# Splitting a 128-place expert's second-stage weights while the 64-place expert behind it runs its first stage

## The chip, the cores and the metric

The kernel runs on one core of a Trainium2 chip. The metric is the device time in microseconds (us) from launch to end, as a median of several runs. An execution under the profiler gives a trace; its span runs from the first to the last instruction. The tensor engine (PE) multiplies, the scalar engine (ACT) and the vector engine (DVE) work on tiles, POOL gathers and scatters rows, and SP issues the weight loads.

## The reference

A two-layer backbone over 256 latent and 256 context tokens: a mixer (convolutions in layer 0, latent attention in layer 1), then a mixture of 16 experts, of which each token takes two.

```
def hier_moe(h, wg, bg, we, be, w1, w3, w2):
    ...
    for e in range(N_EXPERTS):
        hid = jax.nn.silu(t @ w1[e]) * (t @ w3[e])
        out = out + gates[:, e:e + 1] * (hid @ w2[e])
```

D_MODEL is 1024 and D_EXPERT 512, so an expert has 6 MB of weights: w1 and w3 for the first stage, w2 for the second. All is float32.

## The kernel before, in words

The experts of a layer are ranked by the tokens they got and run one after the other. The order of ranks is SEQ; below, a number such as 7 or 8 is the place i in SEQ. The first ranks ("128-place", called B) take up to 128 tokens, the later ones ("64-place", called s) up to 64. In layer 0, places 1 to 10 alternate B, s; then 11 and 12 are B, 13 s, 14 B, 15 s. In layer 1, places 1 to 8 alternate B, s and 9 to 15 are all s. A pair is a B and the s behind it: (1,2), (3,4), (5,6), (7,8), (9,10), (12,13), (14,15) in layer 0 and (1,2), (3,4), (5,6), (7,8) in layer 1.

A B expert multiplies with three products of float32r halves: each weight tile of 1 MB is *split* (L80 to L102) into two column halves, and for each half ACT casts a rounded copy (`wh`, L93) and DVE subtracts it from the source (`wl`, L94). PE then runs `wh` by the high part (L105), `wh` by the low part of the other operand (L106 in the order of the rows) and `wl` by the high part (L107). The split buffers are rings of four `wh` and four `wl` halves, that is of two weight tiles. An s expert multiplies its weights as they are, in float32: L800 in the first stage, L826 in the second.

Each expert has six loads, issued by SP in the order in which the code asks for them: four of the first stage (w1 and w3, two halves of the contraction each) and two of the second (w2). They go into 11 slots of 1 MB, used in turn (`wr` 7 of them, `wx` 4), so that a load waits until the slot's last user, a split or the last L800 or L826 of a tile, is done.

The loop over i (L987 and on) is staggered: it runs the first stage of expert i (`ffn_in` or `ffn_in_half`), and only then the second stage of i-1 (`out_e(i - 1)`, which calls `down` or `down_half`). In between the four weight tiles of the first stage, a list of steps `between` is run, one behind each tile: first `hid`, the transposed hidden row of i-1 (L773 with ACT's L775 and DVE's L776, or L813 with L815), then the transposes of the tokens of i+1 (L699 with L700, or twice L709 with L711 and L712). The second stage's result is weighted by the gate on ACT in layer 0 (`y`, L933), on DVE in layer 1 (L931), and scattered by POOL. L806 and L807 form the hidden row of an s expert from both banks of its first stage.

What order the instructions of an engine have in the program is decided by a scheduler that goes by the code's order and its own estimate of when things are ready. On the chip each engine keeps that order.

Of the kernel before, what the change touches and what calls it, by code (L numbers as in the profile page):

```python
# [44 lines left out]
def backbone(ctx: ExitStack, tc: tile.TileContext, I, out):  # L45
# [13 lines left out]
    def pt(shape=(128, 512)):  # L59
        return pp.tile(list(shape), F32, name="pt", tag="pt", bufs=2)  # L60

    def py(shape=(128, 512)):
        return pp.tile(list(shape), F32, name="py", tag="py", bufs=2)
# [10 lines left out]
    def scratch(t=None):  # L74

        if t is None:
            t = "wh" if scr_n[0] % 2 == 0 else "wl"
            scr_n[0] += 1
        return ring.tile([128, 1024], F32, name="scr", tag=t, bufs=NSPL)
# [5 lines left out]
    def split(src, n=2048):  # L85

        m = n // 2
        hl = []
        for i in range(2):
            hi = ring.tile([128, 1024], F32R, name="wh", tag="wh", bufs=NSPL)  # L90
            lo = ring.tile([128, 1024], F32R, name="wl", tag="wl", bufs=NSPL)
            x = src[i] if isinstance(src, list) else src[:, i * m:(i + 1) * m]
            S.copy(hi[:, :m], x)  # L93
            V.tensor_tensor(lo[:, :m], x, hi[:, :m].bitcast(F32), op=ALU.subtract)  # L94
            hl.append((hi, lo))

        def at(o, width):
            i, o = divmod(o, m)
            return [t[:, o:o + width] for t in hl[i]]

        return at

    def mm3(ps, a, b, start, stop):

        T.matmul(ps, a[0], b[0], start=start, stop=False)  # L105
        T.matmul(ps, a[1], b[0], start=False, stop=False)  # L106
        return T.matmul(ps, a[0], b[1], start=False, stop=stop)  # L107
# [671 lines left out]
    def down(hT, loads):  # L779

        hh, hl = hT
        po = [py(), py()]
        for kh in range(2):
            cur = split(loads.pop(0)())
            for k in range(2):
                kk = kh * 2 + k
                for h in range(2):
                    o = k * 1024 + h * 512
                    mm3(po[h], (hh[:, kk, :], hl[:, kk, :]), cur(o, 512), kk == 0, kk == 3)
        return po  # L790
# [78 lines left out]
    def overflow(l, R, xg, mp):  # L869

        v = nc.values_load(R.mx[0:1, 0:1], min_val=0, max_val=R.nch * 128)
        with tc.If(v > 128, preferred_fallthrough_block=False):

            R.fill()
            posb = sp.tile([128, 2, R.nch], F32, name="posb", tag="posb")
            idc = mp.tile([128, 2, 1], I32, name="idc")
            gtc = mp.tile([128, 1], F32, name="gtc")
            V.tensor_tensor(posb, R.posk, R.cap, op=ALU.add)
            with tc.For_i(0, R.nch, 1):
                V.tensor_scalar(posb, posb, -128.0, None, op0=ALU.add)  # L880
                t = slots(R, posb, "1")
                with tc.For_i(0, NE, 1) as e:
                    V.tensor_copy(idc[:, 0, :], t.idg[:, bass.ds(e, 1)])
                    V.tensor_copy(idc[:, 1, :], t.ids[:, bass.ds(e, 1)])
                    V.tensor_copy(gtc, t.gate[:, bass.ds(e, 1)])
                    win, wout = weights(l, e, lambda: mp.tile([128, 1024], F32, name="wo", tag="ya", bufs=2), True)
                    gather(R, xg, idc[:, 0, :])
                    xb = list(gather_T(xg, mp))[1]
                    hb = ffn_in(xb, win, lambda: scratch()[:, :FE])
                    scatter(R, weigh(R, down(hidden_T(hb, mp), wout), gtc, scratch()), idc[:, 1, :])  # L890

    def new_hs(mp, l):
        return lambda: mp.tile([128, FE], F32, name="hs", tag="hs", bufs=2 - l)

    def experts(l, R, after, mid=None):
# [3 lines left out]
        with tc.tile_pool(name=f"mp{l}", bufs=1, reuse_waits="tile") as mp:  # L899
# [5 lines left out]
            small = [r >= NBIG[l] for r in seq]  # L905
            gate = lambda i: R.t0.gate[:, seq[i]:seq[i] + 1]

            def gat(i):
                idx = R.t0.idg[:, seq[i]:seq[i] + 1]
                if small[i]:  # L910
                    gather_half(R, XG[i % 2][:, :512], idx)
                else:
                    gather(R, XG[i % 2], idx)

            def tokens_T(i):
                return gather_half_T(R, XG[i % 2][:, :512], mp) if small[i] else gather_T(XG[i % 2], mp)
# [22 lines left out]
            def out_e(i):  # L939
                rows_out(i, (down_half if small[i] else down)(hT.pop(i), wout[i]))  # L940

            win, wout, hs, hT = {}, {}, {}, {}
# [45 lines left out]
            for i in range(1, NE):  # L988
                if i < NE - 1:
                    gat(i + 1)  # L990

                def hid():
                    hT[i - 1] = (hidden_half_T if small[i - 1] else hidden_T)(hs.pop(i - 1), mp)

                between = [hid]
                xs = []
                if i < NE - 1:
                    g = tokens_T(i + 1)
                    step = lambda: xs.append(next(g))
                    between += [step] if small[i + 1] else [step, step]  # L1000
                hs[i] = (ffn_in_half if small[i] else ffn_in)(x, win[i], new_hs(mp, l), between)
                x = xs[-1] if xs else None
                out_e(i - 1)
                if i == 2:

                    for j in range(NLAST):
                        sl = scratch()
                        ps = pt((128, nch, 128))
                        r = seq[NE - NLAST + j]
                        for c in range(nch):  # L1010
                            o = sl[:, c * 128:(c + 1) * 128]
                            if r < NBIG[l]:
                                V.tensor_scalar(o, iot1, R.pe[:, c, r:r + 1], None, op0=ALU.is_equal)
                            else:
                                V.tensor_scalar(o.rearrange("p (h n) -> p h n", h=2), iot64, R.pe[:, c, r:r + 1], None, op0=ALU.is_equal)
                            T.transpose(ps[:, c, :], o, ident)
                        S.copy(selT[:, j, :], ps.rearrange("p c n -> p (c n)"))
# [333 lines left out]
    with tc.tile_pool(name="lp", bufs=1, reuse_waits="tile") as lp:  # L1351
        odd.qc = lp.tile([128, 2, 384], F32, name="qc")
        experts(0, R0, after0, odd_q)
        for g in (1, 2):
            shuffle(1, g)
        R1 = odd_layer(A1, B1)
    experts(1, R1, finish)


# [71 lines left out]
```

## Time and profile before

| what | value |
|---|---|
| time, median of 3 runs | 1008.94 us (1007.98 to 1009.62) |
| the profiled execution's own time | 1010.3 us |
| its span | 1008.5 us |
| PE busy (matmuls) | 911.0 us, 90% |
| DVE busy | 595.8 us, 59% |
| ACT busy | 392.3 us, 39% |
| granted PE clock, mean | 0.959 |
| HBM traffic | 320 GB/s over the span |

The experts of layer 0 lie from about 290 to 570 us of the span and those of layer 1 from about 750 us to the end. A row of the timeline gives the start, the length, the engine, the line and what was done; in brackets, how long the engine had been idle and what ended that. Rows of several instructions (x48) are merged.

### The profile page before, as it was taken

The numbers are of one execution on the slowest core, as the hardware profiler recorded it, in microseconds if no ns is written. First come the engines' busy times: TensorE is split into PE (matmuls) and PEld (weight loads), VectorE is DVE, ScalarE is ACT, GpSimd is POOL, SyncE is SP. The second block draws the span as 40 slices with busy tenths as digits, with TensorE's granted clock in tenths as the row PEclk, the third lists the DMA queues.
The fourth block names the chain that finished last, engine by engine and source line by source line (L and its number), as shares of the span: only waits on it lengthen the run. The fifth ranks groups of instructions, "written<-read, shape, count | busy, mean of one in ns | idle before, by whom it ended". The sixth has DMA issues, their size and how long they took to land. (4 is left out here: it accounts for less than half of the span.)

```text
span 1008.5 us, 13283 instructions
## 1 busy us (share of the span) xinstructions
PE 911.0 (90%) x4885; PEld 615.9 (61%) x4885; DVE 595.8 (59%) x944; ACT 392.3 (39%) x571; POOL 119.2 (12%) x127
## 2 busy tenths in 40 slices
PE   2799999999699999999999989999879999999973
PEld 0466676557587775666665468655667776655530
DVE  2789999345777564455643677675589573530005
ACT  2432211321357564355543257343257453221102
POOL 3000000040112111111001011010121111111000
PEclk9899999989899999999999889999979999999997
DMA  9998897984549999999995674262449999999993
GB/s 363 338 340 304 304 328 312 363 327 169 212 162 419 419 420 418 406 396 405 381 359 202 221 235 137 83 227 87 148 164 405 407 386 417 377 401 418 419 420 142
DMA packets 80681, 313.66 MB, mean 311 GB/s; under 512 B 8603, under 2 KB 32155, under 8 KB 50017
## 3 DMA queue, kind: packets, MB, share of 16 engines
q1 hardware_dynamic: 70032, 290.34, 74.4%
q0 software_dynamic: 6368, 11.78, 3.1%
q10 hardware_dynamic: 4208, 10.61, 2.7%
q8 instruction: 40, 0.66, 0.3%
q14 instruction: 33, 0.26, 0.1%
HBM read 301.56 MB, written 21.23 MB: 320 GB/s over the span
## 5 line engine op out<-in xcount | busy, mean ns | idle before, releaser
L94 DVE TENSOR_TENSOR wl<-wr,wh 128x1024 fp32r<-128x1024 f32 (+2 forms) x172 | 201.1, 1204 | 48.4 <-ACT wh L93 47.0
L93 ACT CAST wh<-wr 128x1024 fp32r<-128x1024 f32 (+2 forms) x172 | 172.7, 1037 | 135.1 <-PE pa L107 51.0
L105 PE MATMUL pa<-wh,xh 128*128 128x512 f32 x224 | 92.8, 414 | 5.6 <-ACT wh L93 5.2
L107 PE MATMUL pa<-wl,xh 128*128 128x512 f32 x224 | 91.2, 408 | 2.6 <-DVE wl L94 2.5
L106 PE MATMUL pa<-wh,xl 128*128 128x512 f32 x224 | 90.4, 404 | 1.2 <-DVE xl L712 1.2
L800 PE MATMUL pa<-wr,xs 128*64 128x256 f32 x720 | 84.0, 382 | 3.8 <-DMA wr<-in_moe_w 3.8
L334 DVE SCALAR_TENSOR_TENSOR ca<-apad,cols,ca 128x512 f32<-128x512 f32 x120 | 84.0, 746 | 0.8
L800 PEld LDWEIGHTS pa<-wr,xs 128*64 128x64 f32 x720 | 49.6, 137 | 32.5 <-DMA wr<-in_moe_w 6.8
L105 PE MATMUL pa<-wx,wh 128*128 128x512 f32 x160 | 63.6, 402 | 3.9 <-ACT wx L234 3.9
L183 PE MATMUL py<-wr,csil 128*32 128x512 f32 x384 | 53.2, 659 | 11.1 <-ACT csil L154 11.1
L106 PE MATMUL pa<-wx,wl 128*128 128x512 f32 x160 | 62.6, 393 | 0.0
L107 PE MATMUL pa<-wx,wh 128*128 128x512 f32 x160 | 62.6, 393 | 0.0
L94 DVE TENSOR_TENSOR wl<-wx,wh 128x1024 fp32r<-128x1024 f32 x44 | 52.1, 1220 | 5.2 <-ACT wh L93 4.5
L105 PEld LDWEIGHTS pa<-wh,xh 128*128 128x128 f32 x224 | 43.3, 193 | 18.0 <-ACT wh L93 8.9
L105 PE MATMUL py<-wh,hTh 128*128 128x512 f32 x112 | 47.1, 420 | 6.3 <-ACT wh L93 6.3
L807 DVE TENSOR_TENSOR hs<-hs,pa 128x256 f32<-128x256 f32 x18 | 7.6, 421 | 76.5 <-PE pa L800 76.5
L93 ACT CAST wh<-wx 128x1024 fp32r<-128x1024 f32 x44 | 44.7, 1051 | 19.8 <-PE pa L106 7.3
L107 PEld LDWEIGHTS pa<-wl,xh 128*128 128x128 f32 x224 | 43.2, 193 | 14.9 <-DVE wl L94 4.2
L800 PE MATMUL pa<-wx,xs 128*64 128x256 f32 x432 | 50.5, 382 | 1.1 <-DMA wx<-in_moe_w 1.1
L106 PEld LDWEIGHTS pa<-wh,xl 128*128 128x128 f32 x224 | 43.3, 193 | 11.2 <-DVE xl L712 1.8
L106 PE MATMUL py<-wh,hTl 128*128 128x512 f32 x112 | 46.0, 411 | 0.0
L105 PE MATMUL pa<-wh,wx 128*128 128x512 f32 (+1 forms) x112 | 42.6, 382 | 0.5 <-ACT wh L93 0.5
(358 smaller groups left out, 1514.2 us busy)
## 6 DMA issues: line engine op xcount, KB each, us to landing
wr<-in_moe_w SPq DMA_DIRECT2D x124, 1024.0 KB, 11.5
wx<-in_moe_w SPq DMA_DIRECT2D x68, 1024.0 KB, 11.9
wr<-in_w_mod SPq DMA_DIRECT2D x48, 1024.0 KB, 9.5
wr<-in_ev_w_in SPq DMA_DIRECT2D x20, 512.0 KB, 5.7
wr<-Y SPq DMA_DIRECT2D x6, 1024.0 KB
wr<-in_ev_w_out SPq DMA_DIRECT2D x4, 1024.0 KB
Y<-xg SPq DMA_DIRECT2D x1, 4096.0 KB
wr<-in_od_w_out SPq DMA_DIRECT2D x4, 1024.0 KB
```

Of the source, the lines that this page charges most:

```text
L93: S.copy(hi[:, :m], x)
L94: V.tensor_tensor(lo[:, :m], x, hi[:, :m].bitcast(F32), op=ALU.subtract)
L105: T.matmul(ps, a[0], b[0], start=start, stop=False)
L106: T.matmul(ps, a[1], b[0], start=False, stop=False)
L107: return T.matmul(ps, a[0], b[1], start=False, stop=stop)
L183: T.matmul(ps[32 * j:32 * j + 32, :], csil[:, l, k, :], w[:, j * 512:(j + 1) * 512], start=k == 0, stop=k == 7)
L334: V.scalar_tensor_tensor(acc, apad[:, bi, :, t:t + 256], col("caw", t * 4 + bi), acc, op0=ALU.mult, op1=ALU.add)
L800: T.matmul(ps[m][64 * h:64 * h + 64, :], x[:, k, kh * 64:kh * 64 + 64], w[:, k * 512 + h * 256:k * 512 + h * 256 + 256], start=kh == 0 and ...
L807: V.tensor_tensor(hs, hs, ps[1], op=ALU.mult)
```

## The change

Where expert i is a 64-place one and expert i-1 a 128-place one, the loop puts two steps into `between`: behind the second weight tile of i's first stage the first w2 tile of i-1 is taken and split, and behind the third tile the second. `down` then finds the finished split in place of the weights. The loads are asked for in that order too: of i the first two tiles, w2's first of i-1, i's third, w2's second, i's fourth; before it was i's four and then the two of w2.

```diff
--- before.py
+++ after.py
@@ -781,7 +781,9 @@
         hh, hl = hT
         po = [py(), py()]
         for kh in range(2):
-            cur = split(loads.pop(0)())
+            cur = loads.pop(0)()
+            if not callable(cur):
+                cur = split(cur)
             for k in range(2):
                 kk = kh * 2 + k
                 for h in range(2):
@@ -998,6 +1000,15 @@
                     g = tokens_T(i + 1)
                     step = lambda: xs.append(next(g))
                     between += [step] if small[i + 1] else [step, step]
+                if small[i] and not small[i - 1]:
+
+                    def early(kh):
+                        at = split(wout[i - 1][kh]())
+                        wout[i - 1][kh] = lambda: at
+
+                    between += [lambda: None] * (3 - len(between))
+                    b1, b2 = between[1:3]
+                    between[1:3] = [lambda: (b1(), early(0)), lambda: (b2(), early(1))]
                 hs[i] = (ffn_in_half if small[i] else ffn_in)(x, win[i], new_hs(mp, l), between)
                 x = xs[-1] if xs else None
                 out_e(i - 1)
```

No instruction is added or left out; the scheduler gives some of them other places. In the changed file the lines behind L784 stand two lines lower (L800 is L802, L806 is L808, L813 is L815, L815 is L817, L933 is L935) and those behind L1000 eleven.

On PE, pair (7,8) of layer 0 before: 8 rows from the transposes of place 9's tokens on. `py` is the second stage of 7, `pa` under L800 the first stage of 8; x8 is one weight tile.

```order
L709 MATMUL pt<-ident,xg_1962 128x128 x4
L800 MATMUL pa<-wr,xs 64x256 x8
L709 MATMUL pt<-ident,xg_1962 128x128 x4
L800 MATMUL pa<-wr,xs 64x256 x24
L813 MATMUL pt<-ident,hs 128x128 x2
L699 MATMUL pt<-ident,xg_1961 128x128 x4
L105 MATMUL py<-wh,hTh 128x512
L106 MATMUL py<-wh,hTl 128x512
```

The same place in the changed kernel:

```order
L709 MATMUL pt<-ident,xg_1962 128x128 x4
L802 MATMUL pa<-wr,xs 64x256 x8
L105 MATMUL py<-wh,hTh 128x512
L106 MATMUL py<-wh,hTl 128x512
L105 MATMUL py<-wh,hTh 128x512
L106 MATMUL py<-wh,hTl 128x512
L107 MATMUL py<-wl,hTh 128x512 x2
L105 MATMUL py<-wh,hTh 128x512
L106 MATMUL py<-wh,hTl 128x512
L802 MATMUL pa<-wr,xs 64x256 x8
L107 MATMUL py<-wl,hTh 128x512
```

Eight of the 24 second-stage matmuls of 7 now stand ahead of the third tile of 8, twelve ahead of the fourth, and four behind it; L813 (now L815) and L699 follow those.

On ACT, the same pair before, from the hidden row of 7 (L775) to the casts of place 9 (`wx`, and the last `wr` ahead of them):

```order
L775 CAST hTh<-pt 128x512
L711 CAST xh<-pt 128x512 x2
L806 ACTIVATE hs<-pa 128x256
L815 COPY hTs<-pt 128x256
L93 CAST wh<-wr 128x1024 x2
L700 COPY xs<-pt 128x512
L93 CAST wh<-wr 128x1024 x3
L933 ACTIVATE y<-py,gate_2095 128x512 x2
L93 CAST wh<-wr 128x1024
L93 CAST wh<-wx 128x1024 x6
```

In the changed kernel:

```order
L775 CAST hTh<-pt 128x512
L711 CAST xh<-pt 128x512 x2
L93 CAST wh<-wr 128x1024 x2
L808 ACTIVATE hs<-pa 128x256
L93 CAST wh<-wr 128x1024 x2
L935 ACTIVATE y<-py,gate_2095 128x512 x2
L93 CAST wh<-wr 128x1024 x2
L817 COPY hTs<-pt 128x256
L700 COPY xs<-pt 128x512
L93 CAST wh<-wx 128x1024 x6
```

The four casts of w2 moved up, two of them ahead of the activation of 8's hidden row and two behind it. The first cast of place 9, which was ahead of the two weightings of 7 (the third of the x3), is now behind them.

On DVE, the last pair of layer 0, (14,15), before; L174 shuffles modulation rows for layer 1 and has nothing to do with the experts:

```order
L776 TENSOR_TENSOR hTl<-pt,hTh 128x512
L807 TENSOR_TENSOR hs<-hs,pa 128x256
L174 STREAM_SHUFFLE modc<-modr 128x512
L94 TENSOR_TENSOR wl<-wr,wh 128x1024 x4
L866 SCALAR_TENSOR_TENSOR xl<-py,gate_2095,xh 128x512 x2
```

In the changed kernel:

```order
L776 TENSOR_TENSOR hTl<-pt,hTh 128x512
L94 TENSOR_TENSOR wl<-wr,wh 128x1024 x2
L174 STREAM_SHUFFLE modc<-modr 128x512
L94 TENSOR_TENSOR wl<-wr,wh 128x1024 x2
L809 TENSOR_TENSOR hs<-hs,pa 128x256
```

Two of the four subtractions of 14's w2 moved ahead of the shuffle, and L807 (now L809) moved behind it and behind the other two.

## Rows read from the trace of the kernel before

**Rows 1.** Windows: stretch, busy us of each engine, granted clock, DMA share, GB/s.

```profile
core 0: us, PE busy (x) PEld busy (x) DVE busy (x) ACT busy (x) POOL busy (x), PEclk, DMA share, GB/s
390.00:545.00 155.00, 143.79 (x716) 97.03 (x714) 83.74 (x83) 81.05 (x103) 16.50 (x16) 0.98 0.96 375
...
880.00:985.00 105.00, 93.57 (x670) 51.59 (x668) 14.76 (x21) 13.26 (x26) 11.21 (x12) 1.00 1.01 413
```

**Rows 2.** PE's waits from 378 to 570 us: total, times, longest.

```profile
PE pa L105 <- ACT wh L93: 5.2, 9, 1.7
PE py L105 <- ACT wh L93: 4.4, 5, 1.4
```

**Rows 3.** Timeline of PE, pair (7,8) of layer 0.

```profile
419.97 5.40 PE L800 MATMUL pa<-wr,xs 128*64 128x256 f32 x48
425.97 0.50 PE L813 MATMUL pt<-ident,hs 128*128 128x128 f32 x2 [0.59 <-DVE hs L807]
426.31 0.65 PE L699 MATMUL pt<-ident,xg 128*128 128x128 f32 x4
427.88 0.50 PE L105 MATMUL py<-wh,hTh 128*128 128x512 f32 x1 [0.92 <-ACT wh L93]
428.21 0.40 PE L106 MATMUL py<-wh,hTl 128*128 128x512 f32 x1
...
436.13 0.50 PE L105 MATMUL pa<-wh,xh 128*128 128x512 f32 x1 [0.67 <-ACT wh L93]
...
446.13 0.40 PE L106 MATMUL pa<-wh,xl 128*128 128x512 f32 x1
446.37 0.40 PE L107 MATMUL pa<-wl,xh 128*128 128x512 f32 x1
```

**Rows 4.** Timeline of ACT, the same pair.

```profile
420.08 0.59 ACT L711 CAST xh<-pt 128x512 fp32r<-128x512 f32 x1 [1.93 <-PE pt L709]
423.69 0.38 ACT L806 ACTIVATE hs<-pa 128x256 f32<-128x256 f32 x1 [3.03 <-PE pa L800]
426.51 0.37 ACT L815 COPY hTs<-pt 128x256 f32<-128x256 f32 x1 [2.43 <-PE pt L813]
426.78 2.00 ACT L93 CAST wh<-wr 128x1024 fp32r<-128x1024 f32 x2
433.88 1.27 ACT L933 ACTIVATE y<-py,gate 128x512 f32<-128x512 f32 x2 [1.78 <-PE py L107]
```

**Rows 5.** Timeline of DVE, the same pair.

```profile
427.86 5.88 DVE L94 TENSOR_TENSOR wl<-wr,wh 128x1024 fp32r<-128x1024 f32 x5 [1.94 <-ACT wh L93]
```

**Rows 6.** Loads and gathers: issues, KB each, median us from issue to landing.

```profile
wr<-in_moe_w SPq DMA_DIRECT2D x124, 1024.0 KB, 11.5
xg<-hmD,idx POOLq DMA_INDIRECT x30, 7.7
```

**Rows 7.** Timelines of PE and ACT, pair (12,13) of layer 0.

```profile
512.70 1.95 PE L800 MATMUL pa<-wx,xs 128*64 128x256 f32 x16
...
512.81 0.59 ACT L711 CAST xh<-pt 128x512 fp32r<-128x512 f32 x1 [1.97 <-PE pt L709]
```

**Rows 8.** Timelines of PE, DVE and POOL, pair (14,15), the end of layer 0's experts.

```profile
543.62 3.67 PE L800 MATMUL pa<-wx,xs 128*64 128x256 f32 x32
...
551.34 0.51 PE L813 MATMUL pt<-ident,hs 128*128 128x128 f32 x2 [0.59 <-DVE hs L807]
553.25 0.50 PE L105 MATMUL py<-wh,hTh 128*128 128x512 f32 x1 [1.41 <-ACT wh L93]
...
564.72 3.65 PE L826 MATMUL py<-wr,hTs 128*64 128x512 f32 x16
...
553.94 0.73 DVE L174 STREAM_SHUFFLE modc<-modr 128x512 f32<-128x512 f32 x1
...
551.10 1.48 POOL L214 PARTITION_BROADCAST wr<-modr  x2 [5.96 <-issue]
```

**Rows 9.** Windows at three places where the granted clock changed.

```profile
516.00:519.60 3.60, 2.08 (x13) 1.43 (x10) 1.16 (x2) 2.09 (x3) 0.00 (x0) 1.00 1.00 362
519.60:523.00 3.40, 3.40 (x10) 2.33 (x9) 3.38 (x4) 3.40 (x5) 0.00 (x0) 0.51 1.03 412
...
553.80:560.60 6.80, 5.85 (x14) 4.13 (x13) 5.24 (x6) 2.24 (x3) 0.10 (x1) 0.50 0.69 263
```

**Rows 10.** The chain that ended last, near the end: start, us, what.

```profile
964.59 20.09 DMA wr<-in_moe_w
984.68 0.14 issue
984.81 1.94 PE py L826 x8
```

## The prediction, made before the changed kernel ran

> **What bounds the kernel now.** I read first which resource is full in the two stretches that the change touches. At the end of layer 1 the transfers are: the DMA share is 1.01 and 413 GB/s move, while PE is busy 93.57 of 105 us [rows 1]; the chain that ended last runs there through a wait of 20.09 us for a weight load, and the last eight matmuls of L826 start when it has landed [rows 10]. In layer 0, from 390 to 545 us, PE is busy 143.79 of 155 us, with the DMA share at 0.96 and 375 GB/s: both are near their limit, and 11.2 us of PE are idle [rows 1]. What PE waits for there is not a load: the largest items are `pa` and `py` matmuls that wait for a cast of ACT, 5.2 us in 9 waits and 4.4 us in 5 [rows 2]. So layer 0 goes by the chain PE, ACT, DVE, PE, and layer 1's end goes by bytes.
>
> The pair (7,8) shows where these waits lie. PE does three tiles of L800 without a pause, then waits 0.59 for `hs`, transposes (L813, L699), waits 0.92 for the first split half of w2, and 0.67 for the first tile of place 9 [rows 3]. ACT explains the 0.92: between the activation of `hs` at 423.69 and the copy at 426.51 it waits 2.43 us for L813, and the two casts stand behind that copy [rows 4]. They could have run much earlier; this idle stretch of ACT is what the change fills. A cast takes 1.00 us (2.00 for two), a subtraction 1.18 (5.88 for five) [rows 4, 5].
>
> **The change, part by part.** Work is only moved. PE's second-stage rows of a pair (24 `py` matmuls) now stand 8 ahead of the third tile, 12 ahead of the fourth, 4 behind it. In layer 0 this happens in the pairs (5,6), (7,8), (9,10), (12,13) and (14,15); in (1,2) and (3,4) the scheduler had the casts and matmuls inside the first stage already, and PE's order stays. Of layer 1's pairs only (5,6) and (7,8) change, long before the loads of the end, which arrive at the pace of the DMA either way: I put them at 0, with half a us either way if the first-stage loads of their s experts, now asked for behind w2, come late.
>
> I walk pair (7,8) on durations from [rows 3 to 5]. The second tile of 8 ends at 421.77 (419.97 plus 16 of the 48 matmuls in 5.40). The casts of w2 stand behind the second copy L711 (it follows the one at 420.08 and ends at 420.67), so the halves are cast at 421.7 and 422.6, and their differences done at 422.9 and 424.1. A 512-wide matmul in a run takes 0.235 (446.13 to 446.37). PE: four to 422.7, 0.2 wait, four to 423.9, third tile 1.8 to 425.7, four more to 426.6. The activation of `hs` (0.38) can begin only at 425.8, and the third cast stands behind it: done at 427.25, so PE waits 0.6. Four to 428.2, wait 0.3 for the difference, four to 429.45, fourth tile to 431.25, last four to 432.2, L813 and L699 (0.34 and 0.65) to 433.15. ACT now has both weightings of L933 (1.27 the pair) ahead of the first cast of place 9; the second weighting needs the last `py` of 432.2 and ends at 433.0, so the cast ends at 434.0 and its difference at 435.3. PE waits 0.9, does two matmuls, waits 0.8, and the other 46 of place 9 end at 446.05. Before it was 446.6 (446.37 and one matmul): 0.55 gained.
>
> Against that stands a cost at each restart: the first wide matmul after a change takes 0.33 (427.88 to 428.21) instead of 0.235 [rows 3]. Four more changes at 0.1 are 0.4 lost; nothing is the bound on the other side. So **+0.15 a pair**, between -0.3 and +0.55. The old waits (0.59, 0.92, 0.67) go, and nearly the same amount comes back (0.2, 0.6, 0.3, 0.9, 0.8). I take this for three pairs: **+0.45**, although (5,6) may give 0.
>
> ACT keeps its order in this: the casts at 426.78 start right behind the copy at 426.51, and the next cast of place 9 could not pass L933 [rows 4]. The Trainium skill says so as a rule ("TensorE: Matmul & The Clock Gate", section "Architectural detail: the array is 16× 32×32, not 1× 128×128"): the queues of ScalarE and VectorE are strictly first in, first out. The trace agrees. Could a ready cast overtake, by estimate 2.3 us of the waits in my walk (0.6, 0.9, 0.8) would go; by the rule, they stay.
>
> Pair (12,13) has a worse start: PE is free at 512.7, when L800's sixteen begin, but w2's casts stand behind two L711 of 0.59 from 512.81 on, so that the first half is there at 514.4: 1.7 us of waiting [rows 7]. What comes behind is as in the walk. About the same stall existed there before, later on, so I put it at **-0.3**, restarts included.
>
> Pair (14,15) ends layer 0 and has no next expert, hence no L933 of a successor to suffer from. Its two middle tiles of 32 matmuls run from 543.62 for 3.67 us [rows 8], to 547.2 with what is due then. Now: eight wide matmuls to 549.1, third tile to 550.9, four to 551.8, activation to 551.3, third cast to 552.3, which is 0.5 of waiting, four to 553.25. Then the difference: on DVE it stands behind the shuffle L174, which before started at 553.94, after POOL's L214, and took 0.73 [rows 8]. So it ends at 554.7 plus 1.18, at 555.8: **2.55 us of waiting that the change brings in**. After that four to 556.8, fourth tile to 558.6, four to 559.5, and with the transposition and copy L826 starts at 561.4, if the clock stays up. Before it was 564.72, after waits of 0.59 and 1.41 and with the clock at 0.50 from 553.8 to 560.6 [rows 8, 9]. If 2.55 us of waiting bring a fall too, the start is at 563.1. The gain is 3.3 or 1.6; less 0.4 of restarts, and nearer the lower end, **+1.8**.
>
> What has cover: the s experts' third and fourth loads, one or two places later in SP's order, land 11.5 us after issue and are used a long way behind that; the token gather of 7.7 us stands behind a scatter that is now later by a few us, and its rows are wanted a pair later [rows 6]. If that cover went, each would cost up to its few us once per pair; PE's waits of before show none of that kind, so 0.
>
> **The clock.** Behind waits of 0.59 and 0.92 near 516 to 519.6 (PE busy 2.08 of 3.6), the granted clock is 0.51 for 3.4 us, that is at the lower of the two levels, 1.2 GHz [rows 9]. A fall so costs half of 3.4: 1.7 us. Yet the same two waits in pair (7,8) brought none [rows 3], and the mean clock from 390 to 545 is 0.98 [rows 1]. The skill has a matching sentence ("TensorE: Matmul & The Clock Gate", section "A second HAM failure mode: psum-queue depth-cycling"): short idles of PE between groups of matmuls can make the clock go back and forth, and each fall is paid again. The rows at 519.6 agree, those of pair (7,8) do not. The waits of the walk are as long and come closer together, so I take one fall more than before: **-1.7**; none and three are the bounds.
>
> **Sum.** 0.45 - 0.3 + 1.8 - 1.7 + 0 = 0.25 us less. On the profiled execution's own 1010.3 us (span 1008.5) that is 1010.05; it lies 1.36 above the median of 1008.94, so the median is forecast at **1008.7**.
>
> **The rivals.**
> A, faster: no added fall, and restarts that cost nothing more than the waits themselves. Then 3 x 0.55 + 0.1 + 2.2 = 3.95: **1005.0**. For it: most pairs of before run at full clock through such waits [rows 1]. Against it: the 0.33 in [rows 3].
>
> B, slower: the clock falls once more in each of the pairs (5,6), (7,8) and (9,10). It happens where the wait behind L933 (0.9 and 0.8 within some 2.5 us) comes a little longer. Three falls cost 5.1, less the 1.95 of the other terms: 3.15 slower, **1012.1**. It decides from three falls on; with two the loss is 1.45 and not measurable. For it: [rows 9]; against: the 0.59 and 0.92 without a fall.
>
> C, the change does nothing: DMA paces layer 0 too. For it the share of 0.96; against, 375 GB/s beside 413 where the DMA does bind [rows 1], and waits that name ACT [rows 2]. **1008.9**.
>
> **How the numbers follow.** 0.2%, or 2.0 us, is about what a measurement of this kernel can tell from no change. The forecast (the walks about right, and no more than two added falls) has 0.38, A 0.26, B 0.28, C 0.08. Forecast and C lie within 0.2%: faster 0.26, same 0.46, slower 0.28. The range reaches to the centres of A and B, some way past each: 1004.8 to 1012.3; the likeliest case alone spans 1007.0 to 1010.6.
>
> **What would show it.** Right: `py` no longer waits long for casts behind L813, but L105 and L107 of the next expert's `pa` wait some 0.8 each behind L933; the second half of `py` waits some 0.6 behind the activation; in the last pair L107 waits over 2 us and the shuffle still starts near 553.9; layer 1's end is still a load's. Wrong: a count of granted-clock falls in layer 0 that differs from before by more than one, waits for loads of third tiles, or a shuffle that is ready earlier.

## The result, and the profile after

The changed kernel is slower: a median of 1013.83 us over 11 runs (1010.09 to 1018.68), against 1008.39 us over 11 of before. The ratio is 1.0051, with a 95% interval from 1.0035 to 1.0066, so 5.1 us are lost. That is outside the forecast range. The execution in the trace took 1012.87 us, with a span of 1011.1.

PE's waits in layer 0's experts after the change (from 285 to 575 us; total, times, longest):

```profile
PE pa L105 <- ACT wh L93: 5.7, 5, 1.7
PE py L105 <- ACT wh L93: 3.1, 6, 1.6
PE pa L107 <- DVE wl L94: 2.1, 4, 0.5
PE pa L1064 <- DVE wr L1046: 2.0, 1, 2.0
PE py L107 <- DVE wl L94: 1.8, 1, 1.8
```

The waits for `hs` ahead of L813 (2.9 us before) are gone, and the `py` matmuls wait less for casts (3.1 us beside 4.4 [rows 2]). But three single waits of 1.6 to 2.0 us are new. Two are in sight on the walk that was forecast (`py` L105 1.6, `py` L107 1.8); the third, L1064 on L1046, is in no step of it.

The pair that was walked, (7,8), on PE after the change; it answers to [rows 3]:

```profile
427.01 1.95 PE L802 MATMUL pa<-wr,xs 128*64 128x256 f32 x16
430.38 0.50 PE L105 MATMUL py<-wh,hTh 128*128 128x512 f32 x1 [0.29 <-ACT wh L93]
...
437.56 0.50 PE L105 MATMUL pa<-wh,xh 128*128 128x512 f32 x1 [1.00 <-ACT wh L93]
438.82 0.50 PE L107 MATMUL pa<-wl,xh 128*128 128x512 f32 x1 [0.53 <-DVE wl L94]
```

The waits forecast were 0.2, 0.6, 0.3, 0.9 and 0.8 us; the trace has 0.29, 1.00 and 0.53. Pair (12,13), PE and then ACT, to be held against [rows 7]:

```profile
515.34 1.95 PE L802 MATMUL pa<-wx,xs 128*64 128x256 f32 x16
517.22 0.75 PE L709 MATMUL pt<-ident,xg 128*128 128x128 f32 x4
519.58 0.50 PE L105 MATMUL py<-wh,hTh 128*128 128x512 f32 x1 [1.62 <-ACT wh L93]
...
518.00 0.59 ACT L711 CAST xh<-pt 128x512 fp32r<-128x512 f32 x1 [1.97 <-PE pt L709]
518.48 2.00 ACT L93 CAST wh<-wx 128x1024 fp32r<-128x1024 f32 x2
```

ACT stands idle for 1.97 us in front of the second copy, with the two casts behind it; PE waits 1.62 for them. The last pair on PE and on DVE, and the end of the layer behind it; it answers to [rows 8]:

```profile
549.31 3.67 PE L802 MATMUL pa<-wx,xs 128*64 128x256 f32 x32
561.39 0.74 PE L107 MATMUL py<-wl,hTh 128*128 128x512 f32 x2 [1.84 <-DVE wl L94]
567.04 1.94 PE L828 MATMUL py<-wr,hTs 128*64 128x512 f32 x8
569.80 1.94 PE L828 MATMUL py<-wr,hTs 128*64 128x512 f32 x8
574.45 1.98 PE L1064 MATMUL pa<-wr,ident 128*128 128x512 f32 x4 [2.04 <-DVE wr L1046]
...
559.51 0.72 DVE L174 STREAM_SHUFFLE modc<-modr 128x512 f32<-128x512 f32 x1
572.51 0.75 DVE L868 SCALAR_TENSOR_TENSOR ya<-py,gate,ya 128x512 fp32r<-128x512 f32 x1 [5.40 <-ACT ya L867]
573.18 2.35 DVE L1046 TENSOR_TENSOR wr<-wr 128x1024 f32<-128x1024 f32 x2
```

DVE adds up the scattered rows of all experts (L1046), and PE needs the sums at L1064. They stand behind the weighting of the last expert (L868, then 5.40 us of idleness in front). Before, one addition was ahead of it, in time that DVE had free, as the same rows of DVE before show:

```profile
564.78 1.22 DVE L1035 TENSOR_TENSOR wr<-wr 128x1024 f32<-128x1024 f32 x1
569.14 0.75 DVE L866 SCALAR_TENSOR_TENSOR ya<-py,gate,ya 128x512 fp32r<-128x512 f32 x1 [3.15 <-ACT ya L865]
569.81 1.22 DVE L1035 TENSOR_TENSOR wr<-wr 128x1024 f32<-128x1024 f32 x1
```

Windows after the change (columns as in [rows 1]), over most of layer 0's pairs, the last pair, and layer 1's end:

```profile
394.00:549.00 155.00, 143.66 (x705) 93.99 (x702) 80.90 (x79) 78.57 (x101) 16.23 (x14) 0.98 0.94 371
549.00:575.00 26.00, 21.62 (x119) 11.59 (x119) 10.38 (x13) 7.51 (x11) 3.79 (x5) 1.00 0.64 221
884.00:987.00 103.00, 94.13 (x666) 50.85 (x662) 13.33 (x21) 11.22 (x24) 11.12 (x11) 1.00 1.01 418
```

In layer 0 PE is as idle as before and the DMA share is lower (0.94 beside 0.96), so transfers are not what was lost to. Layer 1's end is still paced by them. In the last pair the granted clock is 1.00 here; over the like stretch before, 543.0 to 569.5, it is 0.87:

```profile
543.00:569.50 26.50, 22.92 (x119) 13.95 (x118) 9.26 (x12) 7.66 (x11) 3.79 (x5) 0.87 0.52 181
```

Some of these stretches at the lower level stand in nearly every trace of a program, others in one trace and not in the next. To compare kernels I take them out: of each stretch of a trace, half of the time at the lower level (0.50 of full speed) is subtracted. What is left repeats within 0.3 us in four traces of the changed kernel, and within 0.5 us in nearly all others where the program is the same (the 18.7 below is the widest miss). The stretches run from the first L800 of an s expert to the first L800 or L826 of the next step named; for instance (12,13) before is 507.59 to 543.62, 36.03 us, less half of 3.4.

| us at full clock | before | after | both copies late (e9) | one add ahead (e13) | both (e14) |
|---|---|---|---|---|---|
| (5,6), L800 to place 8's L800 | 36.0 | 35.2 | 35.3 | 35.2 | 35.2 |
| (7,8), L800 to place 10's L800 | 34.4 | 34.5 | 34.5 | 34.5 | 34.5 |
| (9,10), L800 to its L826 | 29.3 | 29.6 | 29.8 | 29.8 | 29.8 |
| (12,13), L800 to place 15's L800 | 34.3 | 36.5 | 34.3 | 36.5 | 34.3 |
| (14,15), L800 to its L826 | 17.7 | 17.7 | 18.7 | 17.7 | 18.0 |
| L826 to the first L1085 behind the layer | 13.4 | 16.1 | 16.0 | 13.7 | 13.7 |

Two stretches lose, by 2.2 and 2.7 us. As they ran, the traces show less: from the first L800 of an s expert to the end of the table, layer 0 took 258.9 us before and 260.3 to 260.8 in the four traces of the changed kernel. The table leaves out 5.1 us that the lower clock cost before in the pairs (12,13) and (14,15).

### The profile page after: what moved, and what is told of

Its sections match the earlier page's. It is cut to its first block, busy times and chain, and to the rows that moved or that the text cites. A ratio compares the mean times of both kernels' runs of the same rounds, so it can differ in the third digit from the quotient of the medians.

```text
span 1011.1 us, 13270 instructions
## 1 busy us (share of the span) xinstructions
PE 913.9 (90%) x4885; PEld 613.0 (61%) x4885; DVE 598.9 (59%) x944; ACT 391.9 (39%) x571; POOL 121.0 (12%) x127
## 5 line engine op out<-in xcount | busy, mean ns | idle before, releaser
L105 PE MATMUL pa<-wh,xh 128*128 128x512 f32 x224 | 92.6, 413 | 7.0 <-ACT wh L93 6.6
L107 PE MATMUL pa<-wl,xh 128*128 128x512 f32 x224 | 91.4, 409 | 3.1 <-DVE wl L94 3.0
L802 PE MATMUL pa<-wr,xs 128*64 128x256 f32 x736 | 87.8, 384 | 2.9 <-DMA wr<-in_moe_w 2.8
L802 PEld LDWEIGHTS pa<-wr,xs 128*64 128x64 f32 x736 | 49.7, 137 | 35.0 <-DMA wr<-in_moe_w 5.8
L105 PE MATMUL pa<-wx,wh 128*128 128x512 f32 x160 | 64.1, 406 | 4.5 <-ACT wx L234 4.5
L107 PE MATMUL pa<-wx,wh 128*128 128x512 f32 x160 | 63.0, 395 | 0.0
L94 DVE TENSOR_TENSOR wl<-wx,wh 128x1024 fp32r<-128x1024 f32 x46 | 54.4, 1221 | 6.0 <-ACT wh L93 5.2
L105 PEld LDWEIGHTS pa<-wh,xh 128*128 128x128 f32 x224 | 43.3, 193 | 17.1 <-ACT wh L93 7.7
L107 PEld LDWEIGHTS pa<-wl,xh 128*128 128x128 f32 x224 | 43.3, 193 | 15.9 <-DVE wl L94 6.1
L105 PE MATMUL py<-wh,hTh 128*128 128x512 f32 x112 | 46.2, 412 | 4.8 <-ACT wh L93 4.8
L802 PE MATMUL pa<-wx,xs 128*64 128x256 f32 x416 | 48.6, 382 | 1.1 <-DMA wx<-in_moe_w 1.1
L809 DVE TENSOR_TENSOR hs<-hs,pa 128x256 f32<-128x256 f32 x18 | 7.6, 422 | 66.9 <-PE pa L802 66.9
L107 PE MATMUL py<-wl,hTh 128*128 128x512 f32 x112 | 44.3, 420 | 2.3 <-DVE wl L94 1.8
```

The lines of the kernel that those rows point to most:

```text
L802: T.matmul(ps[m][64 * h:64 * h + 64, :], x[:, k, kh * 64:kh * 64 + 64], w[:, k * 512 + h * 256:k * 512 + h * 256 + 256], start=kh == 0 and ...
L809: V.tensor_tensor(hs, hs, ps[1], op=ALU.mult)
```

## The experiments

**Which part loses.** Theory 1 was that layer 0 costs it all; theory 2 that much of it is lost in layer 1's transfers. The condition in the loop was narrowed:

```diff
-                if small[i] and not small[i - 1]:
+                if l == 0 and small[i] and not small[i - 1]:                    (e1)
+                if l == 1 and small[i] and not small[i - 1]:                    (e2)
+                if l == 0 and i == NE - 1 and small[i] and not small[i - 1]:    (e3)
+                if l == 0 and i < NE - 1 and small[i] and not small[i - 1]:     (e4)
```

> The change in layer 0 alone; layer 1 as before. Theory 1 (the loss of 5 us is made in layer 0: more waits of PE for casts, more falls of the granted clock): +3.5 to +5.5 us. Theory 2 (layer 0 costs only what the two profiles show, about +1.3 us, and the rest is lost in layer 1, whose end goes by bytes): +0 to +2 us.

Measured 1.0041 (1.0022 to 1.006), +4.1 us.

> The change in layer 1 alone. Theory 1: within 1 us of before, since that end is paced by transfers. Theory 2: +3 to +5 us, the reordered loads of the s experts delay the stream of transfers and its end.

Measured 0.9981 (0.9967 to 0.9994), -1.9 us. Theory 2 is out, and so is my 0: layer 1 gains.

> The change in the last pair of layer 0, (14,15), alone. The profile after shows the matmuls of L826 3.4 us earlier against its surroundings, but the residual addition L1035 behind the weighting of the last expert, 2.7 us of that given back: -0.7 us by the profile. My forecast had -1.8 us. A rival: a wait of 2 us for that addition brings the clock down at the layer's end, +1 to +3 us.

Measured 1.0048 (1.0033 to 1.0063), +4.8 us: the way of the rival. This is more than the +3 us that the rival allowed. Its trace has the same 2.04 us wait, and the lower clock behind it (PE's timeline, then the window around it, granted clock 0.74):

```profile
571.30 3.20 PE L1064 MATMUL pa<-wr,ident 128*128 128x512 f32 x4 [2.04 <-DVE wr L1046]
```

```profile
569.40:576.00 6.60, 4.70 (x9) 1.68 (x10) 3.38 (x4) 0.00 (x0) 0.00 (x0) 0.74 0.49 143
```

> The change in layer 0 without the last pair. By the profile after (-0.7, +0.1, +2.0, +0.6 us for its pairs) +2 us. Theory 1 (clock falls come more often than in the one profile): +4 to +6 us. Theory 2: at most +2 us.

Measured 1.0015 (1.0002 to 1.0029), +1.5 us, as theory 2 had it; the stretches of its trace add up to 2.0 (-0.7, +0.1, +0.5, +2.1). So layer 0 loses in two places, the last pair and, of the others, (12,13).

**Loads or splits.** Only the loads are asked for earlier; `down` splits as before:

```diff
-                        at = split(wout[i - 1][kh]())
+                        at = wout[i - 1][kh]()
```

> Only the order in which the loads are asked for is changed; the splits stay where they were in the code. If the order of the loads decides what the scheduler does on PE, ACT and DVE, this kernel is the changed one again: +4 to +6 us. If the place of the splits in the code decides, it stays at 0, within 2 us.

Measured 1.0039 (1.0019 to 1.0059), +3.9 us. Its PE program is that of the changed kernel but for three matmuls, and its waits in layer 0's experts are the same to 0.1 us. What the change really is, then, is an order of loads: with that alone the scheduler moves casts, subtractions and matmuls. Why it does so (by when it thinks the weights are there) is my reading of it, and the other way round (splits moved, loads in the old order) was not run.

**Pair (12,13).** The first try to take the casts out from behind the copies L711 put only the earlier copy behind them (b1, the step behind the second tile):

```diff
+                    def first():
+                        early(0)
+                        with tc.issue_after(cast[0].ins):
+                            b1()
```

> The changed kernel, with ACT's second copy of the next tokens (L711) in pair (12,13) queued behind the two casts of w2 instead of ahead of them; nothing else moves on PE. The changed kernel stands at +5 us over before. Theory 1: pair (12,13) loses its 2.2 us at full clock because the casts stand behind that copy (1.62 us of waiting in the trace after). Then that wait goes and the kernel is at +3 to +3.5 us. Rival: PE's more frequent change between the two tile shapes is what costs; the kernel stays at +5 us.

Measured 1.0014 (0.9991 to 1.0036), but the edit missed: the later copy still stood ahead, and the wait with it (ACT, then PE; lines lie two lower):

```profile
514.40 0.59 ACT L713 CAST xh<-pt 128x512 fp32r<-128x512 f32 x1 [3.84 <-PE pt L711]
514.88 2.00 ACT L95 CAST wh<-wx 128x1024 fp32r<-128x1024 f32 x2
...
515.98 0.50 PE L107 MATMUL py<-wh,hTh 128*128 128x512 f32 x1 [1.62 <-ACT wh L95]
```

So its time says nothing on the wait. It has the changed kernel's program on PE, row for row, and yet a median 3.7 us lower against before; how much of such a difference is the clock is worked out below. The mended edit puts both steps behind the cast:

```diff
+                        def steps():
+                            early(0)
+                            with tc.issue_after(cast[0].ins):
+                                b1()
+                                b2()
+
+                        between[1:3] = [steps, lambda: early(1)]
```

> Mends the run before that meant to take away the 1.62 us wait of pair (12,13) and did not: now both copies of the next tokens (L711) stand behind the two casts of w2, on ACT and DVE; PE keeps its order. Theory 1: the wait for the casts goes, the pair's stretch is 1.5 to 2.2 us shorter at full clock, and the whole is +2.5 to +3.5 us over before (the changed kernel +5, the same kernel by its load order alone +3.9). Rival: the casts are late for another reason (their buffers, the load); the wait stays, +4 to +5 us.

Measured 1.0007 (0.9989 to 1.0026), +0.7 us, which is a larger gain than theory 1 had. The casts now run in ACT's idle time at once behind the hidden row, and the copies behind them (ACT, then PE's first matmul with the cast half):

```profile
509.69 2.01 ACT L95 CAST wh<-wx 128x1024 fp32r<-128x1024 f32 x2
511.58 0.60 ACT L713 CAST xh<-pt 128x512 fp32r<-128x512 f32 x1
513.65 0.59 ACT L713 CAST xh<-pt 128x512 fp32r<-128x512 f32 x1 [1.46 <-PE pt L711]
...
513.37 0.48 PE L107 MATMUL py<-wh,hTh 128*128 128x512 f32 x1
```

PE's 1.62 us are gone, and the stretch is 34.3 us again, as before. Two casts on ACT and two subtractions on DVE are all that changed their place. So theory 1 holds for the wait: neither the buffers nor the load kept the casts, the copy did.

**The layer's end.** The first edit put the weighting of the last expert behind two additions:

```diff
+            with nullcontext() if l else tc.issue_after(added[1].ins):
+                rows_out(NE - 1, po)
```

> The changed kernel, with the weighting of layer 0's last expert on DVE queued behind the residual additions of the first two row blocks. Theory 1: the layer's end loses 2.7 us at full clock because the matmuls with the sums (L1053 before) wait 2.0 us for additions that stand behind that weighting, and falls of the clock behind the wait cost more: +1.5 to +3 us over before. Rival: the loss in the last pair comes from the 1.84 us wait behind the shuffle and the falls after it; +4.5 to +5 us as the changed kernel.

Measured 1.0019 (1.0004 to 1.0035), +1.9 us, as theory 1 had it, but not cleanly: the scheduler then took the third addition ahead of the products with the modulation rows as well, and a new wait stands where the old one was; the stretch stays at 15.8 us. Its PE waits from 545 to 590 us:

```profile
PE pt L1096 <- DVE scr L223: 2.9, 1, 2.9
PE py L107 <- DVE wl L94: 2.0, 1, 2.0
```

> Both of these edits in one kernel. Theory 1: +0 to +1.5 us over before, with layer 1's gain of some 2 us in it. Rival (shape changes and the shuffle): +4 to +5 us.

This is e6 with the edit of e5 that missed: 1.0019 (1.0003 to 1.0034). It repeats e6. Next, the additions made late in the kernel before:

> The kernel before, with the residual additions at layer 0's end on DVE queued behind the weighting of the last expert, as the change happens to put them; the rows behind them shift a little. Theory 1 (this is what the last pair loses): +1.5 to +3 us. Rival (the wait behind the shuffle and the falls it brings): -0.5 to +1 us.

Measured 1.0036 (1.0023 to 1.005), +3.6 us. Here too rows behind it moved (waits of 1.3 us for an addition and 1.3 for `scr`), so it shows that this place is dear, not which wait it is. The clean edit waits for the first addition alone, and one instruction changes its place on one engine; the orders of PE, ACT and POOL are the changed kernel's, row for row:

```diff
-            for c in range(nch):
-                add_rows(c)
-            rows_out(NE - 1, po)
+            added = [add_rows(c) for c in range(nch)]
+            with nullcontext() if l else tc.issue_after(added[0].ins):
+                rows_out(NE - 1, po)
```

> The changed kernel with one instruction moved: the first residual addition at layer 0's end stands on DVE ahead of the last expert's weighting again, as before the change; all else keeps its place. Theory 1 (the layer's end loses 2.6 us at full clock because the sums' matmuls wait 2.0 us for additions behind that weighting): the wait goes, the stretch from L826 to the end of the layer is 1.5 to 2.6 us shorter, and the whole is +1.5 to +3 us over before (the changed kernel +5, its load order alone +4). Rival (L826 in two pieces and the 1.84 us wait behind the shuffle): the stretch keeps its 16 us, +4 to +5 us.

Measured 0.9996 (0.9977 to 1.0014). DVE, then PE:

```profile
563.84 1.22 DVE L1046 TENSOR_TENSOR wr<-wr 128x1024 f32<-128x1024 f32 x1
569.32 0.75 DVE L868 SCALAR_TENSOR_TENSOR ya<-py,gate,ya 128x512 fp32r<-128x512 f32 x1 [4.27 <-ACT ya L867]
569.99 1.22 DVE L1046 TENSOR_TENSOR wr<-wr 128x1024 f32<-128x1024 f32 x1
...
569.04 1.88 PE L1064 MATMUL pa<-wr,ident 128*128 128x512 f32 x4
```

L1064 waits for nothing, the stretch is 13.7 us instead of 16.1, and L826 is still in two pieces, with 1.9 us of waiting behind the shuffle in front of it. So neither of those makes the 2.6 us: the rival is out. The time is 0.4 us under before where I expected 1.5 to 3 us over it, and the gain on the changed kernel is larger than the 2.3 us of the stretch; the rest is clock, as worked out below.

**Do the parts add up?**

> The changed kernel with both causes mended, the copies of the next tokens behind the casts in pair (12,13) and the one addition ahead. By the stretches: -0.7 + 0.1 + 0.5 + 0 + 0 us in layer 0 and -2 us in layer 1: -1 to -2.5 us, faster than before. Rival (costs do not add, or falls of the clock take their place): +0 to +2 us.

Measured 0.9972 (0.9958 to 0.9986): -2.8 us, 1006.25 us in the median, a little past the range. With both places mended the change gains, and this version beats both kernels.

The next three leave pairs out, with `(l or i <= 10)`, `(l or i != 15)` and `(l or i == 6)` in the condition:

> The change without the pairs (12,13) and (14,15) of layer 0: the pairs (5,6), (7,8), (9,10) and layer 1 keep it. By the stretches of the traces at full clock: -0.7, +0.1 and +0.3 us in layer 0, -1.3 us and what the transfers add in layer 1, so -1.5 to -2.5 us, faster than both kernels. Rival (falls of the clock behind the waits in front of the next expert cost in every changed pair): +0.5 to +2 us.

Measured 0.9993 (0.998 to 1.0006), less than the gain expected.

> The change without the pair (14,15) alone. Theory 1 (the last pair costs 2.7 us at full clock and more by falls, alone it cost 4.8): 0 to +1.5 us. Rival (the costs do not add; what the last pair costs another place would cost too): +3 to +5 us.

Measured 1.0005 (0.9989 to 1.002), theory 1.

> Layer 1's part of the change and the pair (5,6) of layer 0, the only pair there that got shorter. By the stretches -0.7 and the -2.2 us measured for layer 1 alone: -2 to -3.5 us, faster than both kernels. Rival (layer 1's gain is hidden by the transfers whenever layer 0 shifts): -1 to +0.5 us.

Measured 0.9993 (0.9983 to 1.0004). The rival's figure, but not its reason: in this run's trace layer 1, from its first L800 to the end, takes 228.3 us, as in e2 (228.8) and unlike before (230.7). In the fifteen traces with layer 1 changed it takes 227.7 to 229.8 us, 228.4 in the mean, in the five with it unchanged 229.2 to 231.3, 230.2 in the mean. So the gain of some 1.7 us is there; whether this kernel loses it again, and where, was not found.

**Where the longest executions lose.** The changed kernel's executions spread over 8.6 us, and its trace is one of the shorter, so it was traced three times more:

> The changed kernel itself, one more trace. Its executions spread from 1010 to 1019 us and the trace at hand is one of the shorter. Theory 1: a long execution (over 1014 us) has the same waits and more stretches at the lower clock, behind the waits that the change brings (pair (12,13), the layer's end): at full clock all stretches stay within 0.5 us of the first trace. Rival: a long execution waits for loads, or has a longer stretch at full clock somewhere else.

> The changed kernel, another trace. Theory 1 has further stretches at the lower clock as the whole difference to the first trace, each 1.7 us; the rival has a stretch that is longer at full clock.

> The changed kernel, another trace. Theory 1 has further stretches at the lower clock as the whole difference to the first trace, each 1.7 us; the rival has a stretch that is longer at full clock or a wait for loads.

The three took 1009.68, 1012.15 and 1013.53 us. At full clock every stretch of the table is within 0.3 us of the first trace in all three. What differs among the four lies mostly where no instruction was moved: ahead of the first 64-place expert (320.2 to 322.8 us) and in the mixer between the layers (196.6 to 200.4). The short mixer has 10.2 us at the lower clock, the three others 20.5. Ahead of the experts it is not the clock: the shortest front has the most of it, 30.7 us beside 27.3.

None of the three was over 1014 us, but every execution has its mean granted clock on record. The three longest of the changed kernel (1016.74, 1016.76 and 1018.68 us) have 0.959, 0.959 and 0.956, the lowest of all eleven along with one of 1015.06 us. Multiplied by their clock they come to 974 to 975 us, where the mean of all eleven is 975.5. So a long execution has more of the lower clock and is no longer at full clock, as theory 1 had it. Behind which waits it has it, no trace shows.

## Why the prediction was wrong, step by step

**The last pair, +1.8 us gained: the step that failed most.** Its front was right: L826 was forecast 17.8 us behind the start of the tile pair (543.62 to 561.4), and the trace has 17.7 (549.31 to 567.04), with 1.84 us behind the shuffle where 2.55 were forecast. Two things were wrong around it. The sum was held against a before of 21.1 us, of which 6.8 us ran at the lower clock [rows 9], 3.4 us lost: at full clock that is 17.7, so there was nothing to gain but clock. And the walk ended at the start of L826: what stands behind it was put at nothing, without a reason. Behind that, the first residual addition had moved behind the last weighting on DVE, and the matmuls of the sums wait 2.04 us for it: 2.7 us lost, of which moving that one instruction back returned 2.3 (e13). The signs that the prediction names for this pair came true or nearly so: L107 waits 1.84 us where it said over 2, and the shuffle starts 10.2 us behind the tile pair's start, beside 10.3 before. But none of them looks behind L826.

**Pair (12,13), -0.3 us: mis-sized, 2.2 us lost.** The wait was forecast at 1.7 us and is 1.62. What failed is the sentence that "about the same stall existed there before, later on": the waits of before that go (0.59, 0.92, 0.67 and 0.21, 2.39 us) are nearly paid for by the others that come back (0.29, 1.00, 0.53), as in every pair, and the 1.62 comes on top. That makes 1.05 us more of waiting; the rest of the 2.2 was not taken apart. e9 shows that the 1.62 is the copy ahead of the casts. (Of the two copies only the second runs from 512.81 on; the sum to 514.4 counts one, and is right.)

**The pairs (5,6), (7,8), (9,10), +0.45 us: about right.** Against before they are 0.7 us shorter, 0.1 longer and 0.3 to 0.5 longer, some 0.3 us gained or none. In (7,8) the waits fall from 2.4 to 1.8 us, yet the stretch is 0.1 longer: by this estimate the restarts cost some 0.7, where 0.4 was forecast. e4, which holds these and (12,13), measured +1.5 us.

**Layer 1 at 0: not right.** Alone it gained 1.9 us. Before, a wait of 1.9 us for a difference stood in place 7's first stage; after, it is 0.5 (PE's waits from 836 to 884 us, first before, then after):

```profile
PE pa L107 <- DVE wl L94: 1.9, 1, 1.9
```

```profile
PE py L105 <- ACT wh L93: 1.4, 2, 1.1
PE pa L105 <- ACT wh L93: 0.9, 1, 0.9
PE pa L107 <- DVE wl L94: 0.5, 1, 0.5
```

The windows over pair (5,6) and what follows, before and in e2, show the clock:

```profile
840.00:878.00 38.00, 34.42 (x182) 23.25 (x180) 20.11 (x22) 16.05 (x21) 5.10 (x5) 0.96 0.99 396
```

```profile
839.00:876.00 37.00, 34.00 (x182) 21.72 (x180) 20.05 (x21) 15.58 (x21) 4.63 (x5) 1.00 1.00 405
```

All five traces with layer 1 unchanged (before, e1, e3, e4, e12) have a stretch at the lower clock there, none of those with it changed. Over all executions the lower clock cost 3.6 us less in e2 than in before (table below), so this gain is in the main one of clock. That the end is paced by transfers was true. A likely link is that loads wait for slots that PE has to give free (396 GB/s moved there before and 405 in e2), but it was not tried by itself.

**One more fall of the clock, 1.7 us: not borne out as a sum.** The mean granted clock over the executions is 0.962 in both kernels. The mechanism is there (e3, and two of the four traces of the changed kernel, drop behind the 2.04 us wait), but the change also takes falls away, in the last pair's front and in layer 1.

**The whole, split into full clock and lower clock.** Time multiplied by the mean granted clock estimates what an execution would take at full clock; the rest is what the lower clock cost. The estimate takes off too much where the clock is low while PE waits, in all kernels alike. The last two columns are differences of means, in us, over all executions on record, to those of before in the same comparison (for the changed kernel, to the 125 of all comparisons); their standard errors are 0.7 to 1.3 and 0.9 to 1.5:

| kernel | sum of the stretches, one trace | whole at full clock | cost of the lower clock |
|---|---|---|---|
| changed | +4.6 | +5.0 | 0.0 |
| layer 1 alone (e2) | 0.0 | +1.4 | -3.6 |
| last pair alone (e3) | +2.5 | +1.6 | +3.0 |
| casts first, missed (e5) | +5.1 | +4.8 | -3.0 |
| both copies late (e9) | +3.5 | +3.1 | -2.5 |
| one add ahead (e13) | +2.5 | +2.9 | -3.6 |
| both (e14) | +0.6 | -0.9 | -1.9 |

Here the stretches and the whole at full clock agree within 1.5 us, and so they do in e1, e4, e8, e10, e11 and e15. In e6, e7 and e12 they are 2.8 to 3.8 us apart; there rows behind the last weighting moved as well, so that the last stretch does not hold the same work. By this account the changed kernel's 5.1 us are lost at full clock, in the main in the two stretches named; e5 is faster than it by clock alone; and each mend gives back its stretch and some clock besides. At full clock the kernel with both mends is hardly faster than before, and two thirds of its 2.8 us are clock. One fall more, 1.7 us, does not fit the changed kernel (0.0); the last pair alone has it (e3, 3.0).

**What stays open.** Which waits bring a fall and which do not, no run settles; so the clock's part in each kernel is measured and not explained. Nor was found why e15 does not have the 2.6 us that its one pair and layer 1 should gain.

## What to carry to other kernels

A change that moves work earlier has to be followed past the place where its gain is booked: the scheduler that obeyed it here also put one addition behind a late weighting, and this cost more than all the pairs gained. Read the order of every in-order engine up to the next point where all engines meet, and take stretches at a lower clock out of both sides before one trace is held against another. Where a moved instruction is fed by an engine that has idle time, ask what stands ahead of it there: two small edits turned a loss of 5.1 us into a gain of 2.8, and by the estimate above 5.9 us of that are at full clock.

## What the runs showed of the hardware that I had not expected

The same program, with the same waits to within 0.4 us, has the lower clock behind the 2.04 us wait in two of four traces of the changed kernel, and not in the other two. At the front of the last pair, six of the seven traces with the old program there (before, e2, e4, e10, e11, e15; e12 has 3.4) have it for 6.8 us, behind single waits of at most 1.4 us [rows 8, 9]. The new program has none of it there in five traces of thirteen, 3.4 us in seven and 6.8 in e3, although one of its waits is longer, 1.8 to 2.8 us.
